# Small tiles to the right-hand end of SBUF, so that the operands of a one-core transformer kernel begin at multiples of 128 bytes

## The chip, the cores and the metric

The kernel runs on one core of one Trainium2 chip. The metric is device microseconds of one execution. Before the change the median of three runs is 1484.82 us (1483.15 to 1485.38). One further execution was profiled; the rows in this document are from it.

## What is computed

The reference is a transformer of a first block and two further layers, on 256 tokens of width 1024 in float32:

```python
x = first_block(x, mem, positions, ...)     # rmsnorm, wide projection, three attentions, gates, MLP
h = second_block(x, rel_table_2, ...)       # 4 swiglu FFNs, gated spatial mixer, sparse attention
```

Nearly all of its time goes to products of the 256 token rows with weights. In the first block one projection of 1024 to 4,804 columns feeds sliding-window attention, top-k sparse attention and attention to a memory; their outputs are projected, gated by sigmoids, summed and projected again, and an MLP with a squared relu follows. The second block has four feed-forward nets of the form `(silu(x @ w1) * (x @ w3)) @ w2` with 2,816 hidden columns, a mixer with 4,096 hidden columns, and one attention over compressed, selected and windowed keys. A layer norm closes each part.

## The kernel before

**Three products for one.** Every weight and every activation is split in two parts of type float32r: `h` is the rounded value, `l` what is left. A product is the sum of three matmuls, `h*h`, `h*l` and `l*h` (`mm3`, lines 273 to 277; `down`, lines 304 to 311). The array of TensorE holds one operand still (128 columns of it, the *stationary* one, loaded before each matmul) and streams the other through (256 or 512 columns, the *moving* one).

**The weights' way.** `Stream` (lines 95 to 174) loads halves of weight pieces of 512 KB through SP's queue into five buffers `wr0` to `wr4`. `prep` casts a half on ACT into a buffer `wh` (line 142), and subtracts on DVE into its partner `wl` (line 149). The pairs form a ring: `prep` takes the oldest pair and puts it at the end (lines 139 and 140). There are six pairs, `wh0`/`wl0` to `wh5`/`wl5`, up to the end of the attentions of the first block, and nine from there on: line 758 adds `wh6` to `wh8` in pools of their own, and from then the ring turns as 6, 7, 8, 4, 5, 0, 1, 2, 3. So the pair that a matmul reads follows from counting the casts of line 142.

**Three forms of matmul.** *Up* (`up`, line 279): the weights stand still, the activations of all 256 tokens (`big`, in one place `med`) move; 256 columns. *Row* (`row`, line 294): the activations stand still and the weights move, 256, 452 or 512 columns. *Down* (`down`, line 304, and `down_last`, line 313): hidden activations in tiles `t2` stand still and the weights move, 512 columns, in `down_last` also 256. Nearly the whole kernel after the first attentions is a turn of up, up, down. Transposes (lines 405, 497, 597, 681, 724, 799) stream the identity `ident`, the first 128 columns of tile `cst`, through standing data.

**Where tiles lie.** Memory of a partition is handed out pool by pool in the order in which pools are opened (lines 188 to 195 and 749 to 759), each tile at the next multiple of 32 bytes; a pool that is closed gives its place to the next. The places (bytes from the start of a partition, and what is left after division by 128) come from these sizes, the first pool standing behind 1,152 bytes of the framework's own:

```
pool          first tile at   mod 128
raw  wr0-4          1,152        0
whi  wh0-5         21,632        0
wlo  wl0-5         46,208        0
cp   cst           70,784        0      (257 columns, 1,028 bytes; then two small tiles)
bp   big           72,032       96
mp   med          137,568       96
sm   small        158,048       96
b1                161,696       32      (first block; t2 of the first block behind it, at 64)
t2   t2           161,696       32      (after it)
whi2 wh6-8        184,224       32
wlo2 wl6-8        196,512       32
p2                208,800       32
```

Inside tiles all operands of the float32r matmuls start at multiples of 128 bytes, but for the second half of a 452-column piece. So a matmul of form up has its two operands 96 bytes apart, counted modulo 128, where the weights are in pairs 0 to 5, and 64 apart in pairs 6 to 8; form down 96 apart or 0; form row 32 apart or 64.

**The order of the work.** A scheduler of the framework sorts instructions of an engine unless lines ask for program order (`manual`, `pin`, `first`, `weave`). A tile is written when the last reader of what lay in its place is done. The hand-over from the first block's pools (`b1` and its `t2`) to the second's (`t2`, `whi2`, `wlo2`, `p2`) is in `blocks`, lines 749 to 760.

Of the kernel before, what the change touches and what calls it, by code (L numbers as in the profile page):

```python
# [23 lines left out]
F32 = mybir.dt.float32  # L24
F32R = mybir.dt.float32r
I32 = mybir.dt.int32
# [150 lines left out]
class Ker:  # L177
# [7 lines left out]
    def run(self, stop=None):  # L185
        self.stop = stop
        with ExitStack() as es:
            P = lambda n, b=1, **k: es.enter_context(self.pool(n, b, **k))
            self.W = Stream(self.nc, P("raw"), P("whi"), P("wlo"), self.specs, self.pin)
            self.cp = P("cp")  # L190
            self.bp = P("bp", 8)
            self.mp = P("mp", 5)
            self.sm = P("sm", 6)
            self.ps = P("ps", 4, space=bass.MemoryType.PSUM)
            self.dp = P("dp", space=bass.MemoryType.DRAM)
            self.blocks()
        return self.W.specs
# [345 lines left out]

    def rope_tables(self, p, pos):
        nc = self.nc
        posf = p.tile([128, 2], F32, name="posf")
        self.pin(nc.vector.tensor_copy(posf, pos))
        r = p.tile([128, 2, 32], F32, name="ang")
        q = p.tile([128, 2, 32], F32, name="angq")
        for t in range(2):  # L550
            nc.vector.tensor_scalar(r[:, t], self.cst("inv"), posf[:, t:t + 1], None, op0=OP.mult)
        magic = 12582912.0
        nc.vector.tensor_scalar(q, r, 1.0 / (2 * math.pi), magic, op0=OP.mult, op1=OP.add)
        nc.vector.tensor_scalar(q, q, magic, None, op0=OP.subtract)
        c1 = 6.28125
        c2 = float((np.array(2 * math.pi - c1, np.float32).view(np.int32) & ~np.int32(0xfff)).view(np.float32))
        c3 = float(np.float32(2 * math.pi - c1 - c2))
        for c in (c1, c2, c3):
            nc.vector.scalar_tensor_tensor(r, q, -c, r, op0=OP.mult, op1=OP.add)
        pif = 3.1415925  # L560
        nc.vector.tensor_scalar(r, r, pif, -pif, op0=OP.min, op1=OP.max)
        cosT = p.tile([128, 2, 64], F32, name="cosT")
        sinT = p.tile([128, 2, 64], F32, name="sinT")
        nc.scalar.activation(sinT[:, :, 32:64], r, AF.Sin)
        nc.scalar.activation(q, r, AF.Abs)
        nc.vector.tensor_scalar(q, q, -1.0, math.pi / 2, op0=OP.mult, op1=OP.add)
        nc.scalar.activation(cosT[:, :, 0:32], q, AF.Sin)
        nc.vector.tensor_copy(cosT[:, :, 32:64], cosT[:, :, 0:32])
        nc.vector.tensor_scalar(sinT[:, :, 0:32], sinT[:, :, 32:64], -1.0, None, op0=OP.mult)
        return cosT, sinT  # L570
# [178 lines left out]
    def blocks(self):  # L749
        nc, I = self.nc, self.I  # L750
        with ExitStack() as es:
            p = es.enter_context(self.pool("b1"))
            self.tp = es.enter_context(self.pool("t2", 7))
            R, merge = self.mixers(p)
        es = ExitStack()
        with es:
            self.tp = es.enter_context(self.pool("t2", 11))
            self.W.add(es.enter_context(self.pool("whi2")), es.enter_context(self.pool("wlo2")), 3)
            self.p2 = es.enter_context(self.pool("p2"))
            self.chain(R, merge)  # L760
# [215 lines left out]
    def toeplitz(self):  # L976

        nc, I = self.nc, self.I
        rel = self.p2.tile([32, 16], F32, name="rel")
        nc.scalar.dma_start(rel, I["rel_table_2"])  # L980
        hot = self.med([128, 384])
        self.load_cst(("hot",), hot)
        ps = self.bank()
        nc.tensor.matmul(ps[:16, :384], rel, hot[:32], start=True, stop=True)
        f = self.med([16, 384])
        nc.vector.memset(f[:, 256:], BIG)
        nc.vector.tensor_scalar(f[:, :256], ps[:16, :256], -1.0, None, op0=OP.mult)
        scr = self.dp.tile([16, 384], F32, name="scr")
        nc.scalar.dma_start(scr, f)
        out = []  # L990
        for i in range(2):
            tp = self.big([128, 8, 256])
            if not self.dry:
                src = bass.AP(tensor=scr.tensor, offset=scr.offset + i * 8 * 384, ap=[[1, 128], [384, 8], [1, 256]])
                nc.scalar.dma_start(tp, src)
            out.append(tp)
        return out

    def kv_ffn(self, x, acc):
# [69 lines left out]
        def windows(slot):  # L1069
            T = Ts[slot]  # L1070
            flt = self.med([128, 16, 4, 15])
            if self.dry:
                src = Null()
            else:
                t0 = T[:]
                src = bass.AP(tensor=t0.tensor, offset=t0.offset, ap=[list(t0.ap[0]), [2, 16], [S, 4], [16, 15]])
            pes = pe[:, slot, :, None, None].to_broadcast([128, 16, 4, 15])
            nc.vector.tensor_add(flt, src, pes)
            f = flt.rearrange("p j g n -> p j (g n)")
            nc.vector.memset(fl[slot][:, :, 60:64].bitcast(F32), 0.0)  # L1080
            self.split(fl[slot][:, :, :60], fl[slot][:, :, 64:124], f)

        def compress():
            hid = []
            for s in range(2):
                w1 = I["cmp_w1_2"][s]
                ws = W.get(w1, 0, 8, 0, 256) + W.get(w1, 1024, 8, 0, 256)
                ps = self.bank()
                k = 0
                for wh, wl in ws:  # L1090
                    for i in range(4):
                        f = fl[s][:, k]
                        ops = [(124, wh), (60, wl)]
                        for m, w in ops[::-1] if k == 15 else ops:
                            nc.tensor.matmul(ps[:m, :256], f[:, :m], w[:, i], start=k == 0 and m == 124,
                                             stop=k == 15 and m == 124, skip_group_check=True)
                        k += 1
                r = self.t2([128, 256])
                nc.vector.tensor_copy(r[:124], ps[:124, :256])
                ps = self.bank()  # L1100
                h = self.p2.tile([128, 2, 60], F32, name=f"hid{s}")
                for f in range(2):
                    nc.tensor.matmul(ps[:, f * 60:(f + 1) * 60], r[:124, f * 128:(f + 1) * 128], self.two[:124, :60],
                                     start=True, stop=True)
                for f in range(2):
                    nc.scalar.activation(h[:, f], ps[:, f * 60:(f + 1) * 60], AF.Gelu, bias=self.col("cmp_b1_2", 2 * s + f))
                hid.append(h)
# [21 lines left out]
            for r in range(4):  # L1129
                rs = slice(32 * r, 32 * r + 32)  # L1130
                nc.vector.tensor_copy(self.vc[rs, :, r], ps[rs, :256].rearrange("p (g d) -> p g d", g=4))

        f = self.ffn(x, 1, 0, acc, {1: keys, 2: lambda: windows(0), 3: lambda: windows(1), 4: lambda: key(0), 5: compress, 6: lambda: key(1)})
        for _ in range(3):
            next(f)
# [163 lines left out]
    def mixers(self, p):  # L1299
# [5 lines left out]
        self.c, self.vec, self.vt = {}, {}, []  # L1305
        nc.sync.dma_start(R[:, 0], I["x"][0, :128])
        names = ("ident", "tril_t", "rowok")
        self.load_cst(names, self.cp.tile([128, 257], F32, name="cst"))
        self.ident = self.cst("ident")
        put = [self.vectors(("g_mix", "g_mem"), nc.scalar)]  # L1310
        nc.sync.dma_start(R[:, 1], I["x"][0, 128:])
# [1 line left out]
            for _ in range(4):  # L1313
                W.load()
        self.load_cst(("swa", "causal", "inv"), p.tile([128, 800], F32, name="cstp"))
        pos = p.tile([128, 2], I32, name="pos")
        nc.scalar.dma_start(pos, I["positions"].rearrange("o (t p) -> p (o t)", p=128))
        nr = [self.med([128, D]) for _ in range(2)]
        put.append(self.vectors(("b_gate", "cmp_b1_2"), nc.sync))
# [28 lines left out]
        W.pump()  # L1348
        mem = self.big([128, 2, D])
        nc.sync.dma_start(mem, I["mem"][0].rearrange("(t p) d -> p t d", p=128))  # L1350
        sink = p.tile([128, 8], F32, name="sink")
        nc.scalar.dma_start(sink, I["sinks"].to_broadcast([128, 8]))
        nsink = p.tile([128, 8], F32, name="nsink")
        self.pin(nc.vector.tensor_scalar(nsink, sink, -1.0, None, op0=OP.mult))
        self.cosT, self.sinT = self.rope_tables(p, pos)

# [35 lines left out]
        nc.scalar.copy(vd, PI[:, :, 64:128])  # L1392
        dup = p.tile([128, 2, 2, 64], F32, name="kidup")
        nc.scalar.copy(dup, Ri[:, :, None, 256:320].to_broadcast([128, 2, 2, 64]))
        wi = p.tile([128, 2, 4], F32, name="wi")
        nc.vector.tensor_scalar(wi, PI[:, :, 448:452], 1.0 / 16, None, op0=OP.mult)
        kd = p.tile([128, 2, 64], F32, name="kd")
        self.rope(PI, 0, 1, kd, self.med([128, 2, 64]))
# [184 lines left out]
```

## Time and profile before

| | us |
|---|---|
| median of three runs (lowest, highest) | 1484.82 (1483.15, 1485.38) |
| the profiled execution | 1484.42 |
| its span, first to last instruction | 1482.6 |
| TensorE matmuls busy in it | 1443.6 |
| DVE busy / ACT busy / GpSimd busy | 954.6 / 734.1 / 40.1 |
| mean granted TensorE clock | 0.997 of full speed |

A page and a trace of the profiled execution were read. "Busy" is the time in which an engine executes; matmuls overlap one another, a new one starting while the last is still draining, so the length that a row shows for one matmul (280 ns and more) is not its cost in a stream: that is the time from its start to the next one's start.

### The profile page before, as it was taken

The numbers are of one execution on the slowest core, as the hardware profiler recorded it, in microseconds if no ns is written. First come the engines' busy times: TensorE is split into PE (matmuls) and PEld (weight loads), VectorE is DVE, ScalarE is ACT, GpSimd is POOL, SyncE is SP. The second block draws the span as 40 slices with busy tenths as digits, with TensorE's granted clock in tenths as the row PEclk, the third lists the DMA queues.
The fourth block names the chain that finished last, engine by engine and source line by source line (L and its number), as shares of the span: only waits on it lengthen the run. The fifth ranks groups of instructions, "written<-read, shape, count | busy, mean of one in ns | idle before, by whom it ended". The sixth has DMA issues, their size and how long they took to land.

```text
span 1482.6 us, 25196 instructions
## 1 busy us (share of the span) xinstructions
PE 1443.6 (97%) x10093; PEld 1330.6 (90%) x10093; DVE 954.6 (64%) x1618; ACT 734.1 (50%) x1115; POOL 40.1 (3%) x49
## 2 busy tenths in 40 slices
PE   7899999999999999999999999999999999999997
PEld 6689998989999999889899999999999898899996
DVE  7884488555585455886685454874665778664544
ACT  5564565544354444454354444454654397354442
POOL 0000000000000000100010000100000121100001
PEclk9999999999999999999999999999999999999999
DMA  8453267756556666487546666467665452286650
GB/s 292 129 157 93 65 225 242 223 187 189 171 171 201 192 189 187 138 264 266 157 156 213 186 185 189 134 219 229 219 208 183 125 180 86 67 260 187 185 170 29
DMA packets 191714, 264.81 MB, mean 179 GB/s; under 512 B 11024, under 2 KB 159852, under 8 KB 191596
## 3 DMA queue, kind: packets, MB, share of 16 engines
q1 hardware_dynamic: 183068, 249.56, 53.7%
q10 hardware_dynamic: 8528, 13.64, 3.0%
q8 instruction: 79, 1.29, 0.3%
q14 instruction: 39, 0.32, 0.1%
HBM read 262.09 MB, written 1.07 MB: 177 GB/s over the span
## 4 chain that ended last, share of the span: by engine, by line
PE 83%; DVE 9%; ACT 3%; DMA 2%; issue 2%; DVEq 0%; ACTq 0%
PE acc L311 21%; PE u L275 17%; PE u L276 17%; PE u L277 17%; DVE wl L149 2%; PE acc L695 2%; PE acc L276 1%; PE acc L277 1%; PE acc L275 1%; ACT wh L142 1%; DVE big L850 1%; PE acc L681 1%; DVE bst L379 1%; DMA wr<-in_w_in_dram 1%; DVE big L828 1%
## 5 line engine op out<-in xcount | busy, mean ns | idle before, releaser
L149 DVE TENSOR_TENSOR wl<-wr,wh 128x1024 fp32r<-128x1024 f32 (+3 forms) x488 | 572.6, 1183 | 419.5 <-ACT wh L142 410.6
L142 ACT CAST wh<-wr 128x1024 fp32r<-128x1024 f32 (+3 forms) x488 | 493.3, 1019 | 536.3 <-PE u L276 231.2
L275 PE MATMUL u<-big,wh 128*128 128x256 f32 x1960 | 552.1, 282 | 1.6 <-ACT med L412 1.1
L277 PE MATMUL u<-big,wl 128*128 128x256 f32 x1960 | 550.3, 281 | 0.0
L276 PE MATMUL u<-big,wh 128*128 128x256 f32 x1960 | 550.2, 281 | 0.0
L275 PEld LDWEIGHTS u<-big,wh 128*128 128x128 f32 x1960 | 369.7, 189 | 4.7 <-ACT med L412 1.3
L276 PEld LDWEIGHTS u<-big,wh 128*128 128x128 f32 x1960 | 368.9, 188 | 2.1
L277 PEld LDWEIGHTS u<-big,wl 128*128 128x128 f32 x1960 | 369.6, 189 | 0.0
L311 PE MATMUL acc<-wh,t 128*128 128x512 f32 x928 | 264.0, 395 | 0.0
L311 PEld LDWEIGHTS acc<-wh,t 128*128 128x128 f32 x928 | 169.8, 188 | 35.0
L311 PE MATMUL acc<-wl,t 128*128 128x512 f32 x464 | 145.6, 394 | 0.0
L311 PEld LDWEIGHTS acc<-wl,t 128*128 128x128 f32 x464 | 87.2, 188 | 20.6
L275 PE MATMUL u<-wh,big 128*128 128x256 f32 (+1 forms) x304 | 100.8, 332 | 0.5 <-ACT t L1423 0.5
L277 PE MATMUL u<-wh,big 128*128 128x256 f32 (+1 forms) x304 | 100.5, 331 | 0.0
L276 PE MATMUL u<-wl,big 128*128 128x256 f32 (+1 forms) x304 | 100.0, 329 | 0.0
L331 ACT CAST t<-t 128x512 fp32r<-128x512 f32 x66 | 41.0, 621 | 56.6 <-DVE t L536 25.3
L275 PEld LDWEIGHTS u<-wh,big 128*128 128x128 f32 x304 | 57.1, 188 | 6.9 <-ACT t L1423 0.9
L277 PEld LDWEIGHTS u<-wh,big 128*128 128x128 f32 x304 | 57.1, 188 | 5.5
L276 PEld LDWEIGHTS u<-wl,big 128*128 128x128 f32 x304 | 57.1, 188 | 5.2
L836 POOL TENSOR_TENSOR big<-big,med 128x256 f32<-128x256 f32 x24 | 23.2, 985 | 1384.6 <-ACT big L835 1352.1
L332 DVE TENSOR_TENSOR t<-t,t 128x512 fp32r<-128x512 f32 x66 | 45.3, 686 | 15.1 <-ACT t L331 15.1
L276 PE MATMUL acc<-wl,t 128*128 128x512 f32 (+1 forms) x168 | 53.9, 321 | 0.3 <-DVE wl L149 0.3
(256 smaller groups left out, 1344.3 us busy)
## 6 DMA issues: line engine op xcount, KB each, us to landing
wr<-in_ffn_w_dram SPq DMA_DIRECT2D x264, 512.0 KB, 4.4
wr<-in_w_in_dram SPq DMA_DIRECT2D x34, 512.0 KB, 4.5
wr<-in_w_mlp_in_dram SPq DMA_DIRECT2D x32, 512.0 KB, 4.6
wr<-in_w_mlp_out_dram SPq DMA_DIRECT2D x32, 512.0 KB, 3.9
wr<-in_sgu_w_in_dram SPq DMA_DIRECT2D x32, 512.0 KB, 5.3
wr<-in_sgu_w_out_dram SPq DMA_DIRECT2D x16, 512.0 KB, 5.5
wr<-in_kv_w_dram SPq DMA_DIRECT2D x12, 512.0 KB, 4.4
wr<-in_w_out_dram SPq DMA_DIRECT2D x8, 512.0 KB, 3.8
```

What stands on the lines that cost most here:

```text
L142: self.nc.scalar.copy(h, v)
L149: self.nc.vector.tensor_sub(l, v, h.bitcast(F32))
L275: mm(out, lh, rh, start=start, stop=False, **k)
L276: mm(out, lh, rl, start=False, stop=False, **k)
L277: mm(out, ll, rh, start=False, stop=stop, **k)
L311: mm(acc[t][n], a[:, k, ts], b[:, 0, n * 512:(n + 1) * 512], start=s, stop=e)
L331: self.nc.scalar.copy(h, x)
L332: return self.nc.vector.tensor_sub(l, x, h.bitcast(F32))
L379: b = nc.vector.bn_stats(st[:, 6 * i:6 * i + 6], x[:, c0:c1])
L681: nc.tensor.transpose(pt[:, c:c + 128], e[:, c:c + 128], self.ident)
L695: nc.tensor.matmul(out, PT[:, c:c + 128], v(b), start=b == 0, stop=b == nb - 1)
L836: nc.gpsimd.tensor_mul(x[:, cs], x[:, cs], gB[:, cs])
```

## The change

The pool of small vectors `cp` and that of statistics `sm` are opened on the right-hand side of the memory, that is, from its upper end downward. The constants with the identity get a pool `kp` of their own in the old place, padded from 257 to 288 columns (1,152 bytes, 9 x 128). Odd-sized small tiles of `b1` and `p2` (`pos`, `posf`, `sink`, `nsink`, `wi`, `rel`) move to `cp`, and `hid` is padded from 60 to 64 columns and read as 60. The first block's `t2` is opened before `b1` and no longer behind it. No instruction is added or taken away, and every transfer moves as many bytes as before.

```diff
@@ -187,10 +187,11 @@
-            self.cp = P("cp")
+            self.kp = P("kp")
+            self.cp = P("cp", side="right")
             self.bp = P("bp", 8)
             self.mp = P("mp", 5)
-            self.sm = P("sm", 6)
+            self.sm = P("sm", 6, side="right")
@@ -543,7 +544,7 @@
-        posf = p.tile([128, 2], F32, name="posf")
+        posf = self.cp.tile([128, 2], F32, name="posf")
@@ -749,8 +750,8 @@
+            self.tp = es.enter_context(self.pool("t2", 7))
             p = es.enter_context(self.pool("b1"))
-            self.tp = es.enter_context(self.pool("t2", 7))
@@ -976,7 +977,7 @@
-        rel = self.p2.tile([32, 16], F32, name="rel")
+        rel = self.cp.tile([32, 16], F32, name="rel")
@@ -1098,7 +1099,7 @@
-                h = self.p2.tile([128, 2, 60], F32, name=f"hid{s}")
+                h = self.p2.tile([128, 2, 64], F32, name=f"hid{s}")[:, :, :60]
@@ -1305,7 +1306,7 @@
-        self.load_cst(names, self.cp.tile([128, 257], F32, name="cst"))
+        self.load_cst(names, self.kp.tile([128, 288], F32, name="cst"))
...
```

(`pos`, `sink`, `nsink` and `wi` change from `p.tile` to `self.cp.tile` in the same way.) By the same sizes the first tiles then lie at: `cst` 70,784, `big` 71,936, `med` 137,472, `t2` 157,952, the first block's `b1` 172,288, `wh6` 180,480, `wl6` 192,768, `p2` 205,056. All are multiples of 128, and so is the distance between the two operands of every such matmul, but for that half of the 452-column piece.

## Rows read from the trace of the kernel before

**Rows 1.** The page, parts 1 and 2: busy time of engines, granted clock.

```profile
PE 1443.6 (97%) x10093; PEld 1330.6 (90%) x10093; DVE 954.6 (64%) x1618; ACT 734.1 (50%) x1115; POOL 40.1 (3%) x49
...
PEclk9999999999999999999999999999999999999999
```

**Rows 2.** The page, part 4: chain that ended last, by engine.

```profile
PE 83%; DVE 9%; ACT 3%; DMA 2%; issue 2%; DVEq 0%; ACTq 0%
```

**Rows 3.** The waits: us in total, times, longest us.

```profile
ACT wh L142 <- PE u L276: 231.2, 168, 4.8
```

**Rows 4.** Groups by line and form, engine PE: count | busy us, mean ns.

```profile
L275 PE MATMUL u<-big,wh 128*128 128x256 f32 x1952 | 549.9, 282 | 1.6 <-ACT med L412 1.1 <-DVE nm L671 0.5
...
L311 PE MATMUL acc<-wh,t 128*128 128x512 f32 x928 | 264.0, 395 | 0.0
L311 PE MATMUL acc<-wl,t 128*128 128x512 f32 x464 | 145.6, 394 | 0.0
L275 PE MATMUL u<-wh,big 128*128 128x512 f32 x128 | 51.2, 400 | 0.5 <-ACT t L1423 0.5
...
L275 PE MATMUL u<-wh,big 128*128 128x256 f32 x176 | 49.6, 282 | 0.0
```

**Rows 5.** Timeline of PE, pairs 0 and 1, form up: start us, us.

```profile
501.82 0.28 PE L275 MATMUL u<-big,wh 128*128 128x256 f32 x1
...
507.51 0.40 PE L311 MATMUL acc<-wh,t 128*128 128x512 f32 x1
```

**Rows 6.** Timeline of PE, pairs 6 to 8, form up.

```profile
1389.29 0.28 PE L275 MATMUL u<-big,wh 128*128 128x256 f32 x1
...
1394.73 0.39 PE L311 MATMUL acc<-wh,t 128*128 128x512 f32 x1
```

**Rows 7.** Timeline of PE, pairs 6 to 8, form up, another stretch.

```profile
483.47 0.28 PE L275 MATMUL u<-big,wh 128*128 128x256 f32 x1
...
490.42 0.28 PE L277 MATMUL u<-big,wl 128*128 128x256 f32 x1
```

**Rows 8.** Timeline of PE, pairs 2 and 3, form down.

```profile
490.54 0.63 PE L311 MATMUL acc<-wh,t 128*128 128x512 f32 x2
...
496.14 0.28 PE L275 MATMUL u<-big,wh 128*128 128x256 f32 x1
```

**Rows 9.** Timeline of PE, pairs 6 and 7, form down.

```profile
509.81 1.07 PE L311 MATMUL acc<-wh,t 128*128 128x512 f32 x4
...
512.99 0.28 PE L275 MATMUL u<-big,wh 128*128 128x256 f32 x1
```

**Rows 10.** Timeline of PE, pairs 6 to 8, form down, 256 columns.

```profile
1470.87 0.28 PE L275 MATMUL acc<-wh,t 128*128 128x256 f32 x1
...
1471.95 0.28 PE L275 MATMUL acc<-wh,t 128*128 128x256 f32 x1
```

**Rows 11.** Windows: stretch, us, busy by engine (PE, PEld, DVE, ACT, POOL), clock, DMA.

```profile
152.63:154.76 2.13, 2.13 (x11) 2.13 (x11) 0.42 (x1) 0.37 (x1) 0.00 (x0) 0.50 0.48 162
185.00:212.00 27.00, 27.00 (x214) 26.23 (x214) 23.89 (x42) 19.00 (x35) 0.00 (x0) 1.00 0.63 208
212.00:1475.00 1263.00, 1251.09 (x8712) 1155.26 (x8711) 804.12 (x1226) 609.84 (x848) 37.53 (x42) 1.00 0.59 183
```

**Rows 12.** Timeline of PE, transposes of line 681 in a stream.

```profile
1209.09 0.60 PE L681 MATMUL acc<-cst,t 128*128 128x128 f32 x4
```

**Rows 13.** Preparation of weights, all pairs: ns min/median/max, first and last start.

```profile
L149 DVE TENSOR_TENSOR wl<-wr,wh x488: 295/1225/1667, 14.5 to 1450.6; 128x1024 fp32r<-128x1024 f32 x152, 128x512 fp32r<-128x512 f32 x4, 128x256 fp32r<-128x256 f32 x4, 128x904 fp32r<-128x904 f32 x2
...
L142 ACT CAST wh<-wr x488: 363/1051/1086, 8.4 to 1449.6; 128x1024 fp32r<-128x1024 f32 x152, 128x512 fp32r<-128x512 f32 x4, 128x256 fp32r<-128x256 f32 x4, 128x904 fp32r<-128x904 f32 x2
```

**Rows 14.** Hand-over of the pools: timeline, and line 1545.

```profile
179.33 0.44 PE L724 MATMUL u<-cst,t 128*128 128x128 f32 x2 [0.57 <-DVE t L714]
...
180.07 0.71 ACT L142 CAST wh<-wr 128x256 fp32r<-128x256 f32 x2
...
L1545 DVE TENSOR_TENSOR t<-u,big x12: 677/680/693, 188.3 to 209.8; 128x512 f32<-128x512 f32 x12
```

More of the change, by code (lines that the diff above doesn't have):

```diff
@@ L1315, in mixers @@
         self.load_cst(("swa", "causal", "inv"), p.tile([128, 800], F32, name="cstp"))
-        pos = p.tile([128, 2], I32, name="pos")
+        pos = self.cp.tile([128, 2], I32, name="pos")
         nc.scalar.dma_start(pos, I["positions"].rearrange("o (t p) -> p (o t)", p=128))
@@ L1350, in mixers @@
         nc.sync.dma_start(mem, I["mem"][0].rearrange("(t p) d -> p t d", p=128))
-        sink = p.tile([128, 8], F32, name="sink")
+        sink = self.cp.tile([128, 8], F32, name="sink")
         nc.scalar.dma_start(sink, I["sinks"].to_broadcast([128, 8]))
-        nsink = p.tile([128, 8], F32, name="nsink")
+        nsink = self.cp.tile([128, 8], F32, name="nsink")
         self.pin(nc.vector.tensor_scalar(nsink, sink, -1.0, None, op0=OP.mult))
@@ L1394, in mixers @@
         nc.scalar.copy(dup, Ri[:, :, None, 256:320].to_broadcast([128, 2, 2, 64]))
-        wi = p.tile([128, 2, 4], F32, name="wi")
+        wi = self.cp.tile([128, 2, 4], F32, name="wi")
         nc.vector.tensor_scalar(wi, PI[:, :, 448:452], 1.0 / 16, None, op0=OP.mult)
```

## The prediction

> **What bounds the kernel now.** Read the page first: TensorE is busy for 1443.6 of 1482.6 us, and its granted clock is nine tenths or more in every slice [rows 1]. The chain that ended last agrees, with 83% of it on TensorE [rows 2]. The waits say the same from the other side: what the cast of weights on ACT waits for longest is TensorE, which has to be done with a buffer before it can be filled again [rows 3]. So weights and transfers follow TensorE, and the time falls if matmuls follow each other faster. In the 1,263 us from 212 us on TensorE is busy for 1,251 [rows 11]: there a nanosecond per matmul is worth 99% of itself.
>
> Most matmuls are of two sizes [rows 4]. With 256 columns: 1,952 each at lines 275, 276 and 277 of form up, and 176 each of form row, together 3 x (1,952 + 176) = 6,384. With 512 columns: 928 + 464 of form down and 3 x 128 of form row, 1,776. The 280 and 395 ns that those groups show are lengths with the draining in them; the pace is the time from start to start, and the timeline has it.
>
> **Pace by distance.** Before, the pairs of weights lie at two kinds of places, and the ring tells which pair is at work. Distances of the two operands are modulo 128.
> - 96 apart, pairs 0 and 1, form up: 48 matmuls from 501.82 to 507.51, 5.69 us / 48 = **118.5 ns** [rows 5].
> - 64 apart, pairs 6 to 8, form up: 48 from 1389.29 to 1394.73, **113.3 ns** [rows 6]; but in another stretch 59 from 483.47 to 490.42, **117.8 ns** [rows 7]. Of 24 such stretches of 47 matmuls or more I found 10 at the first pace and 14 at the second, each held to its end. The mean is 0.42 x 113.3 + 0.58 x 117.8 = 115.9.
> - 96 apart, form down, 512 columns: 24 from 490.54 to 496.14, **233.3 ns** [rows 8].
> - 0 apart, form down, 512 columns: 14 from 509.81 to 512.99, **227.1 ns** [rows 9].
> - 0 apart, form down, 256 columns: 9 from 1470.87 to 1471.95, **120.0 ns** [rows 10].
>
> At the half clock (granted 0.50, 1.2 GHz) 10 matmuls of form up, 96 apart, fill 2.13 us (the eleventh in the count is one that drains) [rows 11]: 213 ns, twice 106.7. So at half the pace the distance costs nothing that can be seen; at full clock 7 to 13 ns of a 256-column matmul come on top of 106.7. That is where this change can act.
>
> In the stretch from 212 us on lie 8,712 of 10,093 matmuls [rows 1, 11], and there three pairs of nine are 6 to 8. So about 0.86 / 3 = 29% of each size stand in these pairs now: 1,830 with 256 columns and 510 with 512. The others are 4,554 and 1,266.
>
> **The change, part by part.** No matmul, cast, subtraction or transfer is added or taken out, and no queue gets another order from the code.
>
> *Matmuls.* After the change all the operands are 0 apart, and each starts at a multiple of 128. That last is new: before, every matmul of these forms has at least one operand 32 or 96 off, so no row shows the case. What I take is that 0 and 64 are one class, in which the two reads can fall into step, and 32 and 96 another, in which they can't: rows 6 and 9 against rows 5 and 8. Then the 256-column matmuls of the other pairs come to the mean of the 64-apart stretches, 4,554 x (118.5 - 115.9) = 11.8 us, and the 512-column ones to the 0-apart pace, 1,266 x (233.3 - 227.1) = 7.8 us. Pairs 6 to 8 stay as they are. Sum 19.6 us, of which 99% are on the path: **19.4 us less**. The bounds: every 256-column matmul at the 110 ns of a transposition in a stream (four in 0.60 us, the last 0.27 long, so 0.33 / 3 [rows 12]; this is a short stream behind a full load of standing data) and every 512-column one at twice the half clock's 213 / 2: 4,554 x 8.5 + 1,830 x 5.9 + 1,266 x 20 + 510 x 14 = 82 us less. At the other end 120.0 and 233.3 for all: 4,554 x 1.5 + 1,830 x 4.1 + 510 x 6.2 = 17.5 us more. I take a value near the middle because it rests on the longest stretches.
>
> The Trainium skill, "TensorE: Matmul & The Clock Gate", section "Step-by-step: what each phase is for", says that the standing and the moving operand are read through two independent ports, so that loading the next weights takes nothing from the running matmul. By that rule a distance between the two would not matter, and the sum would be 0. Rows 5 and 6 differ by 5 ns with the same shapes at the same clock, which the rule alone doesn't give; but it is the reason for the second rival below.
>
> *Other matmuls.* The 1,933 that are left are transposes, attention and smaller groups of the forms above. The identity lies at a multiple of 128 before and after. I take 0; if each moves by the 5 ns between rows 5 and 6, that is 10 us either way at most.
>
> *DVE and ACT.* The subtraction takes 1,225 ns and the cast 1,051 ns in the median over all pairs [rows 13]; the rows don't part the pairs, so a gain or a loss of some ns isn't excluded. 0: TensorE covers both as long as ACT waits for it [rows 3]. Without that cover 20 ns on each of 488 subtractions would be 10 us.
>
> *Transfers.* The same bytes into other places; the constants still land as 257 columns. ACT's cast waits mostly for TensorE, so a slower landing would be hidden: 0.
>
> *Hand-over.* The new `t2` now lies on the old `t2`, and `wh6` on tiles of `b1`. The old `t2` is last read by transposes at 179.33 us, and its successor is first written by line 1545 at 188.3 us [rows 14]: 9 us of cover. `wh6` is cast at 180.07, just behind; it can go no later than today, since its new place is free earlier. From 185 to 212 TensorE has no hole (27.00 of 27 us [rows 11]). 0; without that cover a hole of a microsecond.
>
> The profiled execution took 1484.4 us (span 1482.6 and 1.8 around it); 1484.4 - 19.4 = 1465.0. It lies 0.4 under the median of the runs, so I say **1465.4 us**.
>
> **Rivals.**
> - *In step throughout, or better for starting on 128 (faster).* With one distance nothing breaks the faster pace: 113.3 for all 256-column matmuls, 227.1 for the others. 4,554 x 5.2 + 1,830 x 2.6 + 7.8 = 36 us, 1448; if starts at multiples of 128 drop the rest too, down to 1402. For it: a stretch that has the pace holds it [rows 6]. Against: the slower pace is held as well [rows 7]. The Trainium skill, same page, section "Back-to-back issue gap", gives columns / 2.4 GHz plus 2.5 ns, so 109 and 216 ns; the estimate by it is about 1402 us. No row here is at that pace.
> - *Distance isn't it (no change).* The faster stretches belong to pairs 6 to 8 for where they lie in the memory, far above 0 to 5, and that stays. Then 0: 1484.8. For it: the same pairs carry all the fast rows. Against: in these pairs the pace differs between 0 and 64 apart [rows 6, 10], so distance does something.
> - *0 apart is bad for 256 columns (slower).* The only rows with 256 columns at exactly 0 apart run at 120.0 [rows 10], slower than any other. If form up takes that pace, 4,554 x 1.5 + 1,830 x 4.1 - 7.8 = 6.5 us more, **1491**. It decides from 119.0 ns on: today's mean is (4,554 x 118.5 + 1,830 x 115.9) / 6,384 = 117.8, and the 512-column gain pays for 1.2. For it: same distance. Against: stretches of nine matmuls behind others, and both operands 32 off.
> - *It doesn't do what it says* needs a place that misses: only half of the 452-column pieces does, too little for a chance.
>
> **How the numbers follow.** A measurement can tell about 0.2%, 3 us. Forecast (1452 to 1478) 0.38; in step or better 0.22; no change 0.20; slower 0.20. So faster 0.60, same 0.20, slower 0.20. For the range I leave out the lower part of the first rival, below 1425 (about 0.1), and what lies above 1492 (about 0.07); the forecast's own range is 1452 to 1478.
>
> **What would show it.** Right: the timeline of form up with pairs 0 to 5 at 113 to 116 from start to start, 512 columns at 227, for all pairs alike. First rival: 113 or less in all stretches, 216 for 512. Second: 118 with pairs 0 to 5 and 116 with 6 to 8, as now. Third: 120 everywhere with 256 columns. The forecast is wrong altogether if waits of TensorE for weights appear that rows 3 do not have, or if the time changes while these paces don't.

## The result and the profile after

The changed kernel is slower: 1494.57 us in the median of four runs (1492.54 to 1494.87), where the kernel before took 1485.1 us beside it. The ratio is 1.0062, with a 95% interval of 1.0044 to 1.0079. That is 9.5 us more. The forecast was 19.4 us less; the third rival, "0 apart is bad for 256 columns", had the sign and 1491 us. The time lies 2.6 us above the upper end of the range.

The page of the changed kernel, parts 1, 2 and 4 (lines of `kernel.py` are numbered one higher than before from line 190 on):

```profile
PE 1453.2 (97%) x10093; PEld 1342.5 (90%) x10093; DVE 955.0 (64%) x1618; ACT 734.5 (49%) x1115; POOL 40.1 (3%) x49
...
PEclk9999999999999999999999999999999999999999
...
PE 86%; DVE 9%; DMA 2%; ACT 2%; issue 1%; DVEq 0%; ACTq 0%; SPq 0%
```

Beside [rows 1, 2]: the count of matmuls is the same, the granted clock is nine tenths or more in every slice as before, and TensorE is busy for 9.6 us longer, which is the whole loss. DVE and ACT moved by 0.4 us each. So nothing new waits; the same matmuls take longer. The waits and the preparation of weights agree. In the waits of the changed kernel (us in total, times, longest):

```profile
ACT wh L142 <- PE u L277: 235.6, 170, 3.8
```

ACT waits for TensorE 4 us longer than in [rows 3], as it must when TensorE is slower. And the preparation, all pairs (ns min/median/max):

```profile
L149 DVE TENSOR_TENSOR wl<-wr,wh x488: 294/1225/1671, 15.4 to 1458.8; 128x1024 fp32r<-128x1024 f32 x152, 128x512 fp32r<-128x512 f32 x4, 128x256 fp32r<-128x256 f32 x4, 128x904 fp32r<-128x904 f32 x2
...
L142 ACT CAST wh<-wr x488: 364/1051/1089, 8.9 to 1457.7; 128x1024 fp32r<-128x1024 f32 x152, 128x512 fp32r<-128x512 f32 x4, 128x256 fp32r<-128x256 f32 x4, 128x904 fp32r<-128x904 f32 x2
```

The medians, 1,225 and 1,051 ns, are those of [rows 13] to the nanosecond.

The lengths of matmuls hardly show the loss (283 ns against the 282 of [rows 4]); their distance from start to start does. One stretch shows it best, because the program runs the same pieces in the same order in every kernel of this study: between 250 and 300 us there is a form down with pairs 6 to 8 (24 matmuls), and later, one behind the other, a form up with pairs 6 to 8 (48), a form down with pairs 0 to 5 (24) and a form up with pairs 0 to 5 (48). In the timeline of PE of the kernel before, with the first matmul of each piece and the first behind it:

```profile
251.63 0.63 PE L311 MATMUL acc<-wh,t 128*128 128x512 f32 x2
...
257.08 0.28 PE L275 MATMUL u<-big,wh 128*128 128x256 f32 x1
...
279.61 0.28 PE L275 MATMUL u<-big,wh 128*128 128x256 f32 x1
...
285.26 0.63 PE L311 MATMUL acc<-wh,t 128*128 128x512 f32 x2
...
290.86 0.28 PE L275 MATMUL u<-big,wh 128*128 128x256 f32 x1
...
296.55 0.63 PE L311 MATMUL acc<-wh,t 128*128 128x512 f32 x2
```

The same pieces in the timeline of the changed kernel:

```profile
252.72 0.63 PE L312 MATMUL acc<-wh,t 128*128 128x512 f32 x2
...
258.18 0.28 PE L276 MATMUL u<-big,wh 128*128 128x256 f32 x1
...
280.66 0.28 PE L276 MATMUL u<-big,wh 128*128 128x256 f32 x1
...
286.41 0.63 PE L312 MATMUL acc<-wh,t 128*128 128x512 f32 x2
...
291.99 0.28 PE L276 MATMUL u<-big,wh 128*128 128x256 f32 x1
...
297.75 0.63 PE L312 MATMUL acc<-wh,t 128*128 128x512 f32 x2
```

Read each piece as the difference of two starts over its count. Form up with pairs 6 to 8: 5.65 us / 48 = 117.7 ns before, 5.75 / 48 = 119.8 after. Form up with pairs 0 to 5: 5.69 / 48 = 118.5 before, 5.76 / 48 = 120.0 after. Form down with pairs 6 to 8 stays (5.45 and 5.46 us / 24 = 227 ns), and with pairs 0 to 5 it goes only from 5.60 / 24 = 233.3 to 5.58 / 24 = 232.5. The 227 that the forecast gave it did not come.

**All matmuls.** Following the order of the program and counting the casts round the ring gives the two tiles of each matmul, and so its distance. (The ring turns as 6, 7, 8, 2, 3, 4, 5, 0, 1 from where the pools change, not as 6, 7, 8, 4, 5, 0, 1, 2, 3; two casts are sorted ahead of the new pairs there. The matmuls that fall to pairs 6 to 8 are those counted below.) For the sums below I took every interval from one matmul's start to the next that is under 137 ns with 256 columns and 273 ns with 512, that is, those with no wait in them. Distances are the moving operand's start less the standing one's, from here on modulo 256, because with 512 columns 0 and 128 turn out to differ; both are 0 modulo 128.

| form, pairs | intervals | before: distance, mean ns | after: distance, mean ns | us more |
|---|---|---|---|---|
| up, 0 to 5 | 4,191 | 224, 118.34 | 128, 119.09 | 3.1 |
| up, 6 to 8 | 1,816 | 192, 116.23 | 0, 119.67 | 6.2 |
| down 512, 0 to 5 | 1,035 | 224, 233.38 | 128, 232.28 | -1.1 |
| down 512, 6 to 8 | 507 | 0, 228.76 | 0, 229.03 | 0.1 |
| row and down 256, row 512 | 1,377 | several | several | 1.1 |

The sum is 9.5 us before rounding, and 9.5 were measured: the loss is in the paces, two thirds of it in the three pairs that had been the fast ones.

### The profile page after: what moved, and what is told of

The parts are those of the page before. It is cut to its first block, busy times and chain, and to the rows that moved or that the text cites. A ratio compares the mean times of both kernels' runs of the same rounds, so it can differ in the third digit from the quotient of the medians.

```text
span 1490.8 us, 25196 instructions
## 1 busy us (share of the span) xinstructions
PE 1453.2 (97%) x10093; PEld 1342.5 (90%) x10093; DVE 955.0 (64%) x1618; ACT 734.5 (49%) x1115; POOL 40.1 (3%) x49
## 4 chain that ended last, share of the span: by engine, by line
PE 86%; DVE 9%; DMA 2%; ACT 2%; issue 1%; DVEq 0%; ACTq 0%; SPq 0%
PE acc L312 20%; PE u L276 18%; PE u L278 18%; PE u L277 18%; DVE wl L149 2%; PE acc L696 2%; PE acc L277 1%; PE acc L278 1%; PE acc L276 1%; DVE bst L380 1%; DVE big L851 1%; PE acc L682 1%; DVE big L829 1%; PE u L800 1%; ACT wh L142 1%
## 5 line engine op out<-in xcount | busy, mean ns | idle before, releaser
L276 PE MATMUL acc<-wh,t 128*128 128x512 f32 (+1 forms) x168 | 54.1, 322 | 0.0
```

The lines of the kernel that those rows point to most:

```text
L276: mm(out, lh, rh, start=start, stop=False, **k)
```

## The experiments

Four theories stood against each other. **Distance**: the pace follows from how far the two operands' starts are apart, and 0 is bad for 256 columns. **Start**: it follows from where an operand starts, multiples of 128 being bad. **Place**: pairs 6 to 8 are fast because of where they lie. **Hand-over**: the pools' new order costs the time. The edits pad a tile, add an unused one (`pad1` stands ahead of `t2`, `pad2` ahead of `wh6`) or open a pool earlier; no run leaves out any of the work. Where nothing else is said they are made in the changed kernel.

**All operands 64 apart.** The tile of the constants is padded by 64 bytes, which moves everything behind it; a small pool brings pairs 6 to 8 back to a multiple of 128.

```diff
+            es.enter_context(self.pool("pad2")).tile([128, 16], F32, name="pad2")
...
-        self.load_cst(names, self.kp.tile([128, 288], F32, name="cst"))
+        self.load_cst(names, self.kp.tile([128, 304], F32, name="cst"))
```

> Changed kernel with a gap of 64 bytes, so that big, med and t2 lie 64 off a multiple of 128 and all nine pairs of weights at 0: every matmul has its operands 64 apart. Distance theory (only the distance of the two operands modulo 128 sets the pace): the 256-column matmuls run at a mix of 113.3 and 117.8 ns, mean 116.2, the 512-column ones at about 229.8; against before 6,990 x 1.5 + 1,990 x 2.1 = 14.6 us less, about 1470. Start theory (what slows is that operands start at multiples of 128, whatever the distance): activations no longer do, so back to the time before, 1485. Place theory (pace belongs to where a buffer lies in the memory, not to the last bits of the address): as the changed kernel, 1494.

Measured: 1460.72 us, ratio to before 0.9838 (0.9825 to 0.9852), the fastest kernel of the study. Page, part 1, and the same pieces in its timeline:

```profile
PE 1417.2 (97%) x10093; PEld 1309.1 (90%) x10093; DVE 954.7 (65%) x1618; ACT 733.8 (50%) x1115; POOL 39.9 (3%) x49
```

```profile
250.28 0.62 PE L312 MATMUL acc<-wh,t 128*128 128x512 f32 x2
...
255.78 0.28 PE L276 MATMUL u<-big,wh 128*128 128x256 f32 x1
...
277.70 0.28 PE L276 MATMUL u<-big,wh 128*128 128x256 f32 x1
...
283.16 0.62 PE L312 MATMUL acc<-wh,t 128*128 128x512 f32 x2
...
288.66 0.28 PE L276 MATMUL u<-big,wh 128*128 128x256 f32 x1
...
294.12 0.62 PE L312 MATMUL acc<-wh,t 128*128 128x512 f32 x2
```

Form up runs at 5.46 / 48 = 113.8 ns and form down at 5.50 / 24 = 229.2, for all pairs alike, where the changed kernel has 120 and 232.5 or 227.5. TensorE is busy for 36 us less than in the changed kernel, with the same instructions. Only the distance theory had a time below that of the kernel before, and it was 9 us too high: it counted on the mix of 113.3 and 117.8 of the rows, and here 84% of form up's intervals are 113 or 114 ns.

**All 32 off.** The same with 32 bytes of padding, so that form up is 32 apart and the others 96, modulo 128 (160 and 96 modulo 256):

```diff
+            es.enter_context(self.pool("pad2")).tile([128, 24], F32, name="pad2")
...
+        self.load_cst(names, self.kp.tile([128, 296], F32, name="cst"))
```

> Changed kernel with a gap of 32 bytes: form up has its operands 32 apart, forms down and row 96. Distance theory: 256 columns of form up at about 117.2 ns (the rows of form row at 32 apart before), 512 columns at 233.4: against before 7,000 x 0.5 = 3.5 us less and 1,990 x 1.5 = 3 us more, so 1485 within 3. Start theory: 1485 too, as the activations are off 128. Place theory: 1494.

Measured: 1490.15 us, ratio 1.0028 (1.0017 to 1.0040). Its timeline:

```profile
279.50 0.28 PE L276 MATMUL u<-big,wh 128*128 128x256 f32 x1
...
285.20 0.63 PE L312 MATMUL acc<-wh,t 128*128 128x512 f32 x2
...
290.79 0.28 PE L276 MATMUL u<-big,wh 128*128 128x256 f32 x1
...
296.49 0.63 PE L312 MATMUL acc<-wh,t 128*128 128x512 f32 x2
```

5.70 / 48 = 118.8 ns twice and 5.59 / 24 = 232.9. The time lies between the changed kernel and the one before, 5 us above what the distance theory gave: all of form up has a mean of 117.8 where 117.2, from the rows of form row, was expected. So this run fits the theory in direction, not in size.

**Nothing at a multiple of 128.** One unused tile of 32 bytes ahead of all pools: every start is 32 off, every distance stays.

```diff
+            P("pad0").tile([128, 8], F32, name="pad0")
```

> Changed kernel with 32 bytes ahead of everything: no operand starts at a multiple of 128 or 64 any more, all distances stay 0. Distance theory: as the changed kernel, 1494, with 256 columns at 118.5 to 120. Start theory: the slow-down goes, 1485 or less. Place theory: 1494.

Measured: 1493.74 us, ratio 1.0059 (1.0046 to 1.0073), the changed kernel's time. Its timeline:

```profile
280.25 0.28 PE L277 MATMUL u<-big,wh 128*128 128x256 f32 x1
...
286.01 0.63 PE L313 MATMUL acc<-wh,t 128*128 128x512 f32 x2
...
291.58 0.28 PE L277 MATMUL u<-big,wh 128*128 128x256 f32 x1
...
297.34 0.63 PE L313 MATMUL acc<-wh,t 128*128 128x512 f32 x2
```

5.76 / 48 = 120.0 twice, and 5.57 / 24 = 232.1. That the operands begin at multiples of 128, which is what the change was about, is worth nothing either way. The start theory falls. The forecast took the common multiples for a new case, "so no row shows the case"; they made none.

**The pools' order alone**, in the kernel before: `t2` opened ahead of `b1`, nothing else.

```diff
+            self.tp = es.enter_context(self.pool("t2", 7))
             p = es.enter_context(self.pool("b1"))
-            self.tp = es.enter_context(self.pool("t2", 7))
```

> Kernel before with one part of the change alone: the first block's t2 is opened ahead of b1. All distances in the stages after the hand-over are those of before. Distance theory and the prediction's price of 0 for the hand-over: 1485 within 1.5. If the hand-over cost something in the changed kernel, up to 9 us more, with holes of TensorE between 175 and 215 us.

Measured: 1486.07 us, ratio 1.0006 (0.9997 to 1.0014). The hand-over costs nothing that can be told.

**Is the period 128 or 256?** The constants are padded by 192 bytes where the first experiment had 64. Modulo 128 the two are the same kernel; modulo 256 form up of pairs 0 to 5 is 64 apart and no longer 192, and forms down and row of these pairs change from 64 to 192.

```diff
+            es.enter_context(self.pool("pad2")).tile([128, 16], F32, name="pad2")
...
+        self.load_cst(names, self.kp.tile([128, 336], F32, name="cst"))
```

> As d64, with the gap 192 bytes in place of 64: the distance is still 64 modulo 128, but the other of the two values modulo 256. Distance theory with a period of 128: as d64, 1460.7 within 2, form up at 114.1 ns and 512 columns at 229. Rival, a period of 256 or more (in the changed kernel 512-column matmuls of form down ran at 229 with pairs 6 to 8, 0 apart modulo 256, and at 232 with the others, 128 apart): 512 columns up to 3 ns slower or faster, 2,000 x 3 = 6 us, and the 256-column ones up to 4 ns slower, so 1465 to 1490.

Measured: 1475.77 us, ratio 0.9932 (0.9917 to 0.9947), 15 us from its twin. Its timeline:

```profile
252.13 0.63 PE L312 MATMUL acc<-wh,t 128*128 128x512 f32 x2
...
257.64 0.28 PE L276 MATMUL u<-big,wh 128*128 128x256 f32 x1
...
279.90 0.28 PE L276 MATMUL u<-big,wh 128*128 128x256 f32 x1
...
285.37 0.62 PE L312 MATMUL acc<-wh,t 128*128 128x512 f32 x2
...
290.96 0.28 PE L276 MATMUL u<-big,wh 128*128 128x256 f32 x1
...
296.61 0.63 PE L312 MATMUL acc<-wh,t 128*128 128x512 f32 x2
```

Pairs 6 to 8 are still 192 apart in form up and 64 in form down, and run at 5.47 / 48 = 114.0 and 5.51 / 24 = 229.6, like the twin. Pairs 0 to 5 are 64 and 192 apart now, and in this stretch run at 5.65 / 48 = 117.7 and 5.59 / 24 = 232.9. So 128 bytes more matter. With 512 columns it is plain: the same pairs have a mean of 229.0 at 64 in the twin and 233.0 at 192 here.

With 256 columns it is not. Other stretches of pairs 0 to 5 in this kernel, also 64 apart, have the fast pace; the first of these two pieces does not and the second does:

```profile
500.14 0.28 PE L276 MATMUL u<-big,wh 128*128 128x256 f32 x1
...
505.79 0.62 PE L312 MATMUL acc<-wh,t 128*128 128x512 f32 x2
...
516.75 0.28 PE L276 MATMUL u<-big,wh 128*128 128x256 f32 x1
...
522.19 0.62 PE L312 MATMUL acc<-wh,t 128*128 128x512 f32 x2
```

5.65 / 48 = 117.7 and 5.44 / 48 = 113.3 are the two paces that pairs 6 to 8 have at 192 in the kernel before ([rows 7] and [rows 6]). In form up 37% of the intervals are fast (under 114.5 ns) at 64 here, 35% at 192 in the kernel before and 84% at 192 in the twin. So the distance of a matmul's own operands doesn't fix which of the two it gets, and that 64 and 192 differ for 256 columns isn't shown. Whether 256 is the whole period or half of a longer one was not tried.

**Smooth, stepped, or 64 exactly?** The weights are read from 16 bytes into wider tiles, so that form up is 48 apart (d48) or 80 (d80) modulo 128.

```diff
-                new.append((hi.tile([128, 1024], F32R, name=f"wh{k}"), lo.tile([128, 1024], F32R, name=f"wl{k}")))
+                new.append((hi.tile([128, 1056], F32R, name=f"wh{k}"), lo.tile([128, 1056], F32R, name=f"wl{k}")))
...
-            h, l = (x[:, :a // 2 * b].rearrange("p (a b) -> p a b", b=b) for x in buf)
+            h, l = (x[:, 4:4 + a // 2 * b].rearrange("p (a b) -> p a b", b=b) for x in buf)
```

The padding is that of the first experiment for d48, and 96 bytes (312 columns) with a `pad2` of 32 bytes for d80. The wider tiles put every second pair 128 bytes further modulo 256, so each kernel has two distances in form up.

> As d64, with the weights 16 bytes further inside their buffers: form up has its operands 48 apart, forms down and row 80. Distance theory, smooth around 64: 256 columns of form up between the paces at 64 and 32, (114.1 + 117.8) / 2 = 116, 512 columns (229 + 233.2) / 2 = 231: 6,000 x 1.9 + 2,000 x 2 = 15 us over d64, 1476. Rival, in steps of 32 (16 bytes don't count): as one of the neighbours, 1461 or 1490. Rival, 64 exactly is needed: 1485 to 1494.

> As d48 with the gap 96 bytes in place of 64: form up 80 apart, forms down and row 48. Distance theory, smooth around 64: 256 columns of form up between 114.1 and 118.3 (96 apart before), 116.2, 512 columns 231: about 1477. Rivals as for d48.

Measured: 1486.95 us, ratio 1.0008 (0.9998 to 1.0018), and 1491.06 us, 1.0041 (1.0027 to 1.0055). Sixteen bytes off in either direction and the time is that of the kernel before, or above it: nothing is left of the 1.6% that the first experiment gained on it. In the means over all intervals form up has 116.9 at 48 and 118.8 at 176; 118.2 at 80 and 119.1 at 208; the 114.1 that the first experiment had comes back at none of them. A reservation: these weights start 16 bytes off a multiple of 32, which no other kernel here has, so part of it may be the start and not the distance.

**Place.** The kernel before with pairs 6 to 8 pushed up by 96 bytes: they stay in the same region, and lose their good distances (up 192 becomes 96, down 0 becomes 96).

```diff
+            es.enter_context(self.pool("pad2")).tile([128, 24], F32, name="pad2")
```

> Kernel before with 96 bytes ahead of pairs 6 to 8 alone: these weights, too, start at a multiple of 128, and every matmul of the forms up and down is 96 apart, with no pair 64 or 0 apart any more. Distance theory: the fast third of before is lost, 256 columns at 118.4 and 512 at 233.3 for all pairs: 2,100 x 2.0 + 640 x 4.2 = 7 us over before, 1492. Place theory (pairs 6 to 8 are fast for where they lie): 1485.5, as before.

Measured: 1494.55 us, ratio 1.0063 (1.0048 to 1.0078): one unused tile, and the kernel before loses what the change lost (1492 was expected of the distance theory). Its timeline:

```profile
252.74 0.63 PE L311 MATMUL acc<-wh,t 128*128 128x512 f32 x2
...
258.34 0.28 PE L275 MATMUL u<-big,wh 128*128 128x256 f32 x1
...
280.95 0.28 PE L275 MATMUL u<-big,wh 128*128 128x256 f32 x1
...
286.71 0.63 PE L311 MATMUL acc<-wh,t 128*128 128x512 f32 x2
...
292.32 0.28 PE L275 MATMUL u<-big,wh 128*128 128x256 f32 x1
...
298.00 0.63 PE L311 MATMUL acc<-wh,t 128*128 128x512 f32 x2
```

Pairs 6 to 8 go from 117.7 to 5.76 / 48 = 120.0 ns and from 227.1 to 5.60 / 24 = 233.3; pairs 0 to 5, untouched, keep 5.68 / 48 = 118.3. The place theory falls.

**The change without its distances.** All of the change, and three paddings that give the operands the distances of the kernel before (`pad2` stands ahead of the second block's `t2` here).

```diff
+            es.enter_context(self.pool("pad1")).tile([128, 16], F32, name="pad1")
...
+            es.enter_context(self.pool("pad2")).tile([128, 16], F32, name="pad2")
...
+        self.load_cst(names, self.kp.tile([128, 312], F32, name="cst"))
```

> Changed kernel, with gaps that give big, med, t2 and pairs 6 to 8 the distances from one another and from pairs 0 to 5 that they had before, modulo 256; everything else of the change stays (pools on the right-hand side, the identity's pool, the order of t2 and b1, the padded hid). Distance theory: the time before, 1486 within 2. Rival, something else of the change costs: between that and 1494.

Measured: 1485.82 us, ratio 1.0000 (0.9991 to 1.0010). The same pieces:

```profile
279.44 0.28 PE L276 MATMUL u<-big,wh 128*128 128x256 f32 x1
...
285.10 0.63 PE L312 MATMUL acc<-wh,t 128*128 128x512 f32 x2
...
290.70 0.28 PE L276 MATMUL u<-big,wh 128*128 128x256 f32 x1
...
296.38 0.63 PE L312 MATMUL acc<-wh,t 128*128 128x512 f32 x2
```

5.66, 5.60 and 5.68 us, the lengths of before. What the change does besides, the sides of the memory, the moved small tiles and the order of pools, costs nothing that can be told. `big` and `med` also lie at their old starts again, so this run alone doesn't part distance from start; the run with everything 32 off does that. The two together put the loss down to the distances.

**Whose weights?** While a matmul streams, the next weights are loaded. Is it the matmul's own standing operand whose distance counts, or the next one's? Only `wl` is moved, so that the two answers differ: it begins 64 bytes inside tiles that are widened by 128. By that, `wl` lies in form up 64 or 192 apart, modulo 256, by turns from tile to tile.

```diff
+                new.append((hi.tile([128, 1024], F32R, name=f"wh{k}"), lo.tile([128, 1056], F32R, name=f"wl{k}")))
...
+            h, l = (x[:, o:o + a // 2 * b].rearrange("p (a b) -> p a b", b=b) for x, o in zip(buf, (0, 16)))
```

> Changed kernel, with the rests of the weights (wl) 64 bytes inside their buffers, the rounded weights (wh) where they were. In form up the matmuls of line 276 and 277 have wh standing, those of line 278 wl. Own theory (what counts is a matmul's moving operand against its own standing one): line 278 runs at 113 to 117, lines 276 and 277 at 119 to 120. Next theory (it counts against the operand that is being loaded for the next matmul meanwhile): line 277 runs at 113 to 117, the others at 119 to 120. By either a third of 6,000 gains 3 to 5 ns: 6 to 10 us under the changed kernel, 1485 to 1489.

Measured: 1483.5 us, ratio 0.9983 (0.9973 to 0.9993), 11 us under the changed kernel and a little under the forecast. The three matmuls of form up (lines 276 to 278) come out at 117.3, 117.7 and 117.9 ns in the mean by line, where either answer wanted one that stands apart. But these means mix the two distances of `wl`. Apart, in pairs 6 to 8, the three lines have 118.7, 120.6 and 113.6 ns where `wl` is 64 apart (some 190 intervals each), as the matmul's own operand would have it, and 118.0, 117.4 and 118.6 where it is 192 apart (some 390 each), with line 277 lowest, as the next one's would. Neither answer holds for both, so the question stays open.

**The paces as a check on all of them.** For each kernel but the one with the pools' order alone the intervals of its groups, by their means against the means of before, give a sum that should be the measured difference:

| kernel | sum of the paces, us | measured (medians), us |
|---|---|---|
| the change | 9.5 | 9.5 |
| 64 apart | -28.3 | -24.8 |
| 192 of padding | -12.7 | -10.6 |
| 32 apart | 5.3 | 4.6 |
| 48 / 80 apart | 2.8 / 5.8 | 0.6 / 4.7 |
| before, pairs 6 to 8 moved | 10.1 | 8.2 |
| everything 32 off | 9.3 | 8.2 |
| the change without its distances | 0.0 | -0.3 |
| `wl` moved | -1.4 | -2.6 |

(For instance 64 apart: 1,816 x (114.08 - 116.23) + 4,191 x (114.08 - 118.34) = -21.8 us for form up, -4.4 for form down with 512 columns, -2.2 for the rest.) Signs agree, and so does the order but among the slowest three, which lie within 1.3 us. The sums run some 2 to 4 us off where much changes; where those microseconds go was not looked into.

## Why the prediction was wrong

**What held.** TensorE sets the time, and a nanosecond per matmul is worth nearly itself. DVE, ACT, transfers and the hand-over were costed at nothing; they came at nothing (the medians of the preparation, the run with the pools' order alone, the change without its distances). No wait for weights appeared. That distance matters was right, and the run 64 apart shows that it moves the time by more than the forecast had it: 24.8 us below the kernel before.

**The step that failed** is the sentence "What I take is that 0 and 64 are one class, in which the two reads can fall into step, and 32 and 96 another". It failed twice.

- *For 256 columns.* The gain of 11.8 us came from giving 0 apart the mean of the 64-apart stretches, 115.9. At 0 and 128 the means are 119.67 and 119.09: form up of pairs 0 to 5 lost 3.1 us where nearly all of the 11.8 was booked, and "pairs 6 to 8 stay as they are" lost 6.2 us more. The evidence was at hand: [rows 10], 256 columns at exactly 0 apart, run at 120.0, and the text set them aside because the stretches were short and both operands 32 off. The run with everything 32 off shows that this second reason weighs nothing.
- *For 512 columns.* The gain of 7.8 us came from [rows 9], 227.1 at 0 apart. But pairs 0 to 5 came to lie 128 apart, which the working modulo 128 calls 0, and that distance runs at 232.28: the gain was 1.1 us. This also keeps the third rival short. It had the right mechanism and took this gain in full: 1491 + 6.7 would have been 1498, less the 256-column matmuls that stayed a little under 120.0 ((119.09 - 120.0) x 4,191 = -3.8 and (119.67 - 120.0) x 1,816 = -0.6): 1493.3, close to the 1494.57 measured.

The two slips differ. For 256 columns 0 and 128 are both slow, so counting modulo 128 did no harm there; putting 0 beside 64 did. For 512 columns 0 and 64 are alike (228.8 and 229.8 in the kernel before), as the sentence has it; putting 128 beside 0 did the harm. That the classes were made modulo 128 was a choice which no row supported. The starts in bytes stood in the table of places, and modulo 256 the rows of before would have been 224 and 192 (form up), 224 and 0 (form down), with no 128 among them. The honest bound would have been that no row shows pairs 0 to 5 at their new distance, with 512 columns as with 256. A smaller slip: the sum took the 256-column matmuls of form row, 32 apart, at form up's 118.5; the kernel before has them at 117.2 in pairs 0 to 5 (387 intervals), half a microsecond in all.

The break-even of that rival, a mean of 119.0 ns for 256 columns, was set with the whole 512-column gain; without it, it is nearer to 118. The mean over all 7,000 intervals with 256 columns after the change is 119.2, against 117.7 before.

The Trainium skill, "TensorE: Matmul & The Clock Gate", section "Step-by-step: what each phase is for", has the two operands read through independent ports, and the second rival drew on it. No change of distance would then move the time. One tile of 64 bytes more and another of 64 moved it by 34 us, so for the pace of these matmuls the measurements decide against that conclusion; whether it is the ports that collide, no run shows. The same page's section "Back-to-back issue gap" gives columns / 2.4 GHz plus 2.5 ns for a matmul alone, an estimate of 109 and 216 ns here, and says that in a stream of loads and matmuls both set the spacing. Of whole pieces of form up and form down none is faster than 113.3 [rows 6] and 226.7 ns (24 matmuls from 456.83 to 462.27 us in the kernel before).

## What to carry to other kernels

Where TensorE is the bound and both operands of a matmul come out of the same memory, read the pace from start to start, sort it by the distance between the two operands' starts, and treat padding as a knob to be tried: here two paddings took the changed kernel from 1494.57 to 1460.72 us, and one unused tile cost the kernel before 8.2. Alignment to a round number is no aim in itself; the round number put all operands on the two distances that are slow for 256 columns. When a class of cases is made up for a forecast, look whether the rows would still fit with another modulus, and believe the one row that has the exact new case over a mean of many that only resemble it.

## What was not expected of the hardware

- The distance counts modulo 256 at least with 512 columns: pairs 0 to 5 have 229.0 ns at 64 (1,345 intervals of the kernel 64 apart) and 233.0 at 192 (1,347 of the one padded by 192), and after the change 0 has 229.0 and 128 has 232.3 in form down.
- With 256 columns the fast pace, 113 or 114 ns, makes up a third of form up or more at 64 and at 192, and at most 2% at 0, 96, 128, 160 and 224. At 48, 80, 176 and 208 it makes up at most 4%, with the reservation on the start made above, and the means are 116.9, 118.2, 118.8 and 119.1.
- At 64 and 192 each piece of form up has one of two paces, 113 to 114 or near 118. It is not chance: of the 22 pieces that lie wholly in pairs 6 to 8, the same 8 are fast in the kernel before, with the pools' order alone, and in the change without its distances. So something else in the order of the program or in the distances of the neighbours tips a piece. What it is, and which two reads collide, no run here settles.
